# A fifth Strassen block pair in ten of the eleven gate and up tiles of a decoder layer's second FFN, with its weight sums made during keys and queries

## The chip, the core and the metric

The kernel runs on one core of one Trainium2 chip, with float32 inputs and outputs. The metric is the device time of one execution in microseconds; the time before is the median of three runs. Five engines matter in the text: PE (TensorE, matmuls), DVE (VectorE), ACT (ScalarE), POOL (GpSimd, which here issues transfers and does a few small operations) and SP (SyncE, which issues most transfers). Each runs its own instructions in order; semaphores tie them together.

## The reference

One layer of a decoder with 256 tokens and 16 meta tokens ahead of them, width 2048. What the change touches is the last line; keys and queries are part of `mixer`.

```python
h = h + 0.5 * swiglu(rms_norm(h, g1), w_gate1, w_up1, w_down1)   # D_FF = 5632
u = rms_norm(h, g_mix)                                           # mixer: attention + short conv
h = h + merged(u) @ w_out
h = h + 0.5 * swiglu(rms_norm(h, g2), w_gate2, w_up2, w_down2)
# swiglu(x, g, u, d) = (silu(x @ g) * (x @ u)) @ d
```

## The kernel before

**Products.** Each weight block comes from memory in float32. ACT copies it to a rounded high half `whi` (line 175), DVE subtracts this from the block and so makes the low half `wlo` (line 176). A product is then three matmuls: high by high, high by low, low by high (lines 374 to 376, 402 to 404 and 408 to 410). `Stream` (class at line 105) keeps all weights in one list: loads of up to 1 MB into `raw` buffers (issued by SP at line 152), and splits of up to 1024 columns. One split is one **step**: `next` runs what is due at the step, makes the split three steps ahead, runs what is due behind it (`waiting`), and hands out the blocks. Functions are put in with a step number by `later`, `early` and `put`, so that number sets the order on DVE, ACT and POOL. There are four buffers for split halves, so the split of step n+4 waits until PE has used that of step n. In the second FFN there are four raw buffers (`raw` three times, `raws` once); a load goes out when the load four places ahead has been split.

**Stages.** First FFN; keys and values (steps 0 to 9 of the second stage), index queries (10 to 25), queries (26 to 41); convolution, eight columns of six steps each (from 42); gates and branches; output product; second FFN. While the convolution runs, the steps' list also holds the top-k selection (`top`), the queries' scaling and rotation (`scaled`, `rotation`), the turn of the queries into the tile `qT` (line 1135) and the scores (line 1208).

**Second FFN.** The tokens are two halves of 128; gate and up weights come in tiles of 512 + 512 columns, 6 in the first group and 5 in the second (`GROUPS`), each followed by its down product in two halves. A tile runs over 2048 inputs as eight **pairs** of 128-row blocks, counted from 0. A plain pair is 2 steps of four products (24 matmuls). A Strassen pair (`MIXED`, in tiles other than the first: 1, 3, 5 and 6) is 4 steps, A, B, C, D, with 2, 1, 2 and 2 products (21 matmuls): seven products of sums of token halves with sums of weight blocks. A and B use three of the four weight blocks as they are (a load of 768 KB), C and D use four sums of weight blocks (a load of 1 MB). The sums of activations lie in tiles such as `comb`; `act_combos` makes them.

**Weight sums.** The sums are made ahead of time by **jobs** (`job`, lines 554 to 573): POOL loads 1 MB, DVE makes four sums of 128x512 in place, one at a step, POOL stores the result to a scratch tensor (`made`, or `sums` for down weights). 46 jobs run during the first FFN, the other 11 during gates and branches, every 5 or 6 steps.

**Between tiles.** The gated result of a tile is turned block by block (`turn_gated`), stored to `hold`, read back as `mt` in four pieces of 128 KB by POOL's queue (`move_blocks`, lines 645 and 648) while the next tile runs, and split into `mid`.

`FIVE` lists the tiles in which pair 4 (`FIFTH`) is a Strassen pair, too; before, it is empty.

Of the kernel before, what the change touches and what calls it, by code (L numbers as in the profile page):

```python
# [9 lines left out]
F32 = mybir.dt.float32  # L10
# [59 lines left out]
FIFTH = 4  # L70
FIVE = ()
LAST_MORE = 3, 4
JOBS_FROM = 24
JOBS_EVERY = 5
JOBS = 46
LATE_FROM = 4
LATE_EVERY = 6
# [5 lines left out]
    act_combos=(4, 12, 19, 32), factors=(7, 10, 12), out=(1, 1, 5, 17), act_split=(9, 14, 25, 33),  # L83
    below=(12, 17, 22, 30, 34), below_split=(15, 20, 30, 34, 35), fifth=(22, 25), late_below=(0, 5),
    late_split=(0, 6),
# [150 lines left out]
def tile_decoder_layer(  # L236
# [316 lines left out]

    def job(pool, bufs, src, to, at, every, touch):
        box = {}

        def load():
            box["x"] = pool[0].tile([P, RAW], F32, name="made", bufs=bufs)
            if touch:
                nc.vector.tensor_copy(box["x"][:, :1], ones[:, :1])  # L560
            nc.gpsimd.dma_start(box["x"], src)

        def sums(n):
            b12, b11, b22, b21 = (box["x"][:, i * HALF : (i + 1) * HALF] for i in range(4))
            to, a, b, op = (
                (b22, b22, b12, "sub"), (b12, b12, b11, "sub"), (b11, b22, b11, "add"), (b21, b21, b11, "sub")
            )[n]
            getattr(nc.vector, f"tensor_{op}")(to, a, b)  # L568

        st.later(load, 1, at)  # L570
        for n in range(4):
            st.later(lambda n=n: sums(n), 1, at + every + n)
        st.later(lambda: nc.gpsimd.dma_start(to, box["x"]), 1, at + every + 4)

    def ffn_features():
# [3 lines left out]
        with tc.tile_pool(name="ffn1", bufs=2, reuse_waits="tile") as fp:  # L579
# [15 lines left out]

            for i, (src, to) in enumerate(made[:JOBS]):
                job([fp], 3, src, to, st.at + JOBS_FROM + i * JOBS_EVERY - 1, JOBS_EVERY, i < 3)

# [55 lines left out]
    def ffn_tokens():  # L654

        with ExitStack() as pools:
# [209 lines left out]
            for g, n in enumerate(GROUPS):  # L866
                for f in range(n):
# [11 lines left out]
                    if (g, f) == (g, 1 - g) and any(at[0] == g for at in FIVE):  # L879
                        written.discard("fifth")  # L880
                        fns = combos(halves, FIFTH, [below[:, 1, :1], below[:, 0]], "fifth")
                        put(fns, 5 * (LAG["fifth"][0],) + 4 * (LAG["fifth"][1],))
                    quads(c, m, lambda k, j, part: known(("act", k // 4), act_tokens(k, j, part)), now, 8, lambda m=m: put(spread(m), LAG["spread"]))
# [67 lines left out]
    with ExitStack() as mix:  # L951
# [6 lines left out]
        qiT = mp.tile([P, 8, SEQ], F32, name="qiT", tag="tA")  # L958
        qT = mp.tile([P, H, SEQ], F32, name="qT", tag="tB")
        ys = mp.tile([P, H, 2, SEQ], F32R, name="ys")  # L960
        cs = [mp.tile([P, KC // 2, 2, SEQ], F32R, name=f"cs{i}", tag=f"c{i}") for i in range(2)]
        vts = mp.tile([P, 4, G * HD], F32, name="vts", tag="vts")
# [239 lines left out]
        def scores(p, lag):  # L1202
            px = aux_tile("psc")
            for a in range(2):
                hh = 2 * p + a
                for j in (1, 2):
                    at = META * (2 - j)
                    nc.tensor.matmul(
                        px[:, a, SIDE[j]],
                        qT[:, hh, (j - 1) * P : j * P],  # L1210
                        kall[:, hh // (H // G), at : at + SEEN[j]],
# [69 lines left out]


        def q_steps():
            left = len(steps)
# [11 lines left out]
            new += [prep[3], tops[3], prep[4], tops[4], visit(prep[5], tops[5]), tops[6]]  # L1296
            new += [visit(*[lambda j=j: turn(qT, j) for j in (1, 2)]), tops[7], mask]
            for i in range(left):
# [46 lines left out]
        def conv_b(c, pb, y):  # L1345
            t = mw.tile([P, SEQ], F32, name="t", tag="cy")
            joined(t, pb)
            nc.vector.tensor_mul(y, t, y)
            to = cs[c // 4][:, c % 4]
            split_into(to[:, 0, :], to[:, 1, :], y)  # L1350

        for c in range(KC):
            box = {}
# [21 lines left out]
        st.later(jobs_pool, 3)  # L1375
        for i, (src, to) in enumerate(made[JOBS:]):
            job(jobs, 2, src, to, st.at + LATE_FROM + i * LATE_EVERY, LATE_EVERY, i < 2)

# [236 lines left out]
```

## Time and profile before

| what | us |
|---|---|
| median of three runs | 2108.76 (2107.89 to 2109.12) |
| span of the profiled execution | 2106.9 |
| PE busy in it | 2098.8 |
| DVE busy | 1582.4 |
| ACT busy | 1058.9 |
| keys to the last convolution column | 788 to 1070 |
| gate and up tiles and down products of the second FFN | 1419 to 2101 |

The profile records one execution; the span goes from its first to its last instruction. A row of a timeline gives the start, the duration, the engine, the line and the operation, with what ended the idle time ahead of it in brackets. A row of a windows' view gives PE, weight loads, DVE, ACT and POOL in this order, busy us with the number of instructions, then PE's clock (1.00 throughout), the mean share of the DMA engines and GB/s. A row of issues gives the size and the median time from issue to landing. Matmuls overlap, so the distance of two starts is less than a matmul's duration.

### The profile page before, as it was taken

Reading aid. Unit: us, or ns where it says so; the run is one execution under the profiler, and the core shown is the slowest. Engines: PE = TensorE matmul, PEld = TensorE weight load, DVE = VectorE, ACT = ScalarE, POOL = GpSimd, SP = SyncE. Lnnn points to the kernel's source line nnn. Section 1 sums busy time; section 2 is a strip of 40 time slices with the busy share of each in tenths; the row PEclk is TensorE's granted clock in tenths of the full one; section 3 lists DMA queues with packets and bytes.
Section 4 is the critical chain, followed back from the end, with each engine's and each line's share of the span. In section 5 each row is a group of like instructions: output and inputs, shape, how many; then the busy total and the mean of one; then the engine's idle time right before and its main releaser. Section 6 shows DMA issues by size and latency. Waiting matters only on the chain.

```text
span 2106.9 us, 31863 instructions
## 1 busy us (share of the span) xinstructions
PE 2098.8 (100%) x12731; PEld 1889.9 (90%) x12731; DVE 1582.4 (75%) x2144; ACT 1058.9 (50%) x1342; POOL 106.0 (5%) x207
## 2 busy tenths in 40 slices
PE   9999999999999999999999999999999999999998
PEld 9999999999999999889988888888888888888887
DVE  7676766676776766578679678769788896878897
ACT  6444433344444445565444444456575565566654
POOL 0000000000000000000000000011000000000000
PEclk9999999999999999999999999999999999999999
DMA  7788888888888865445468886667988777799865
GB/s 265 260 320 327 324 315 322 311 337 310 322 313 325 328 224 177 164 159 181 152 216 329 323 301 223 219 233 255 314 314 300 281 268 247 282 306 319 306 250 207
DMA packets 85908, 575.64 MB, mean 273 GB/s; under 512 B 10112, under 2 KB 10880, under 8 KB 23808
## 3 DMA queue, kind: packets, MB, share of 16 engines
q1 hardware_dynamic: 64080, 438.34, 58.4%
q0 software_dynamic: 21104, 134.23, 17.1%
q8 instruction: 99, 1.62, 0.3%
q10 hardware_dynamic: 576, 1.05, 0.1%
q14 instruction: 49, 0.40, 0.1%
HBM read 504.90 MB, written 68.68 MB: 272 GB/s over the span
## 4 chain that ended last, share of the span: by engine, by line
PE 98%; DVE 1%; DMA 1%; issue 0%; ACT 0%; DVEq 0%; ACTq 0%
PE three L409 5%; PE three L408 5%; PE three L410 5%; PE pd L375 4%; PE pd L376 4%; PE pd L374 4%; PE pu L374 4%; PE pg L375 4%; PE pg L374 4%; PE pu L375 4%; PE pg L376 4%; PE pu L376 4%; PE pgt L402 3%; PE pgt L404 3%; PE pgt L403 3%; PE one L408 3%
## 5 line engine op out<-in xcount | busy, mean ns | idle before, releaser
L176 DVE TENSOR_TENSOR wlo<-raw,whi 128x1024 fp32r<-128x1024 f32 (+1 forms) x771 | 906.2, 1188 | 464.5 <-ACT whi L175 457.7
L175 ACT ACTIVATE whi<-raw 128x1024 fp32r<-128x1024 f32 (+1 forms) x771 | 786.4, 1030 | 883.4 <-PE pd L375 146.2
L375 PE MATMUL pd<-mid,whi 128*128 128x272 f32 x704 | 201.9, 287 | 0.0
L376 PE MATMUL pd<-mid,wlo 128*128 128x272 f32 x704 | 201.9, 287 | 0.0
L374 PE MATMUL pd<-mid,whi 128*128 128x272 f32 x704 | 201.9, 287 | 0.0
L374 PE MATMUL pu<-act,whi 128*128 128x272 f32 x672 | 192.8, 287 | 0.0
L376 PE MATMUL pu<-act,wlo 128*128 128x272 f32 x672 | 192.7, 287 | 0.0
L376 PE MATMUL pg<-act,wlo 128*128 128x272 f32 x672 | 192.7, 287 | 0.0
L375 PE MATMUL pg<-act,whi 128*128 128x272 f32 x672 | 192.7, 287 | 0.0
L375 PE MATMUL pu<-act,whi 128*128 128x272 f32 x672 | 192.7, 287 | 0.0
L374 PE MATMUL pg<-act,whi 128*128 128x272 f32 x672 | 192.7, 287 | 0.0
L568 DVE TENSOR_TENSOR made<-made 128x512 f32<-128x512 f32 x228 | 156.3, 685 | 0.0
L408 PE MATMUL three<-whi,act 128*128 128x512 f32 x352 | 137.2, 390 | 0.1
L409 PE MATMUL three<-wlo,act 128*128 128x512 f32 x352 | 137.0, 389 | 0.0
L410 PE MATMUL three<-whi,act 128*128 128x512 f32 x352 | 137.0, 389 | 0.0
L376 PEld LDWEIGHTS pd<-mid,wlo 128*128 128x128 f32 x704 | 132.7, 188 | 0.0
L374 PEld LDWEIGHTS pd<-mid,whi 128*128 128x128 f32 x704 | 132.7, 188 | 0.0
L375 PEld LDWEIGHTS pd<-mid,whi 128*128 128x128 f32 x704 | 132.7, 188 | 0.0
L176 DVE TENSOR_TENSOR wlo<-raws,whi 128x1024 fp32r<-128x1024 f32 x92 | 103.5, 1140 | 31.7 <-ACT whi L175 31.0
L374 PEld LDWEIGHTS pu<-act,whi 128*128 128x128 f32 x672 | 126.7, 188 | 0.0
L374 PEld LDWEIGHTS pg<-act,whi 128*128 128x128 f32 x672 | 126.7, 188 | 0.0
L376 PEld LDWEIGHTS pg<-act,wlo 128*128 128x128 f32 x672 | 126.6, 188 | 0.0
(381 smaller groups left out, 4482.7 us busy)
## 6 DMA issues: line engine op xcount, KB each, us to landing
raw<-in_wgu_dram SPq DMA_DIRECT2D x123, 1024.0 KB, 6.4
raw<-in_wd_dram SPq DMA_DIRECT2D x63, 1024.0 KB, 6.7
made<-in_wgu_dram POOLq DMA_DIRECT2D x41, 1024.0 KB, 10.6
made<-made POOLq DMA_DIRECT2D x41, 1024.0 KB, 6.5
raw<-made SPq DMA_DIRECT2D x31, 1024.0 KB, 6.1
raw<-in_wcv_dram SPq DMA_DIRECT2D x24, 1024.0 KB, 4.9
raw<-in_wgc_dram SPq DMA_DIRECT2D x24, 1024.0 KB, 5.1
raw<-in_wga_dram SPq DMA_DIRECT2D x24, 1024.0 KB, 5.4
```

The costliest lines, as they stand in the source:

```text
L175: nc.scalar.activation(hi[:, :n], raw, AF.Copy)
L176: nc.vector.tensor_sub(lo[:, :n], raw, hi[:, :n].bitcast(F32))
L374: nc.tensor.matmul(ps, whi, xhi, start=first, stop=False)
L375: nc.tensor.matmul(ps, whi, xlo, start=False, stop=False)
L376: nc.tensor.matmul(ps, wlo, xhi, start=False, stop=last)
L402: nc.tensor.matmul(ps, xhi, whi, start=k + i == 0, stop=False)
L403: nc.tensor.matmul(ps, xhi, wlo, start=False, stop=False)
L404: nc.tensor.matmul(ps, xlo, whi, start=False, stop=k + i == n - 1)
L408: nc.tensor.matmul(ps, x(0), w[0], start=first, stop=False)
L409: nc.tensor.matmul(ps, x(0), w[1], start=False, stop=False)
L410: nc.tensor.matmul(ps, x(1), w[0], start=False, stop=last)
L568: getattr(nc.vector, f"tensor_{op}")(to, a, b)
```

## The change

`FIVE` now lists the tiles 1 to 5 of the first group and all five of the second, so pair 4 of these tiles is a Strassen pair, and the Strassen pairs of a tile are 1, 3, 4, 5, 6. That makes ten more jobs. The list of jobs stays in the order of use: the first 46 still run in the first FFN, the last 11 during gates and branches, and ten in between now run from step 3 of the second stage, one every five steps. Job i (from 0) loads at step 3 + 5i, makes its sums at steps 8 + 5i to 11 + 5i, and stores at step 12 + 5i. Its buffer is the place of the tile `cs1` (even i, tag c1) or of `qT` (odd i, tag tB); these tiles are now created when they are first written, `qT` at step 58 and `cs1` in the convolution's fifth column. The activations' sums for pair 4 go into `below`; their nine operations (five adds, two ACT copies, two subtractions) are put at other steps of the first tile that needs them.

```diff
-FIVE = ()
+FIVE = (*((0, f) for f in range(1, GROUPS[0])), *((1, f) for f in range(GROUPS[1])))
...
+MID_JOBS = 10
+MID_FROM = 3
+MID_EVERY = 5
...
-    below=(12, 17, 22, 30, 34), below_split=(15, 20, 30, 34, 35), fifth=(22, 25), late_below=(0, 5),
+    below=(12, 17, 22, 30, 34), below_split=(15, 20, 30, 34, 35), fifth=(5, 5, 7, 7, 9, 11, 11, 13, 13), late_below=(0, 5),
...
-    def job(pool, bufs, src, to, at, every, touch):
+    def job(place, src, to, at, every, touch):
...
-            box["x"] = pool[0].tile([P, RAW], F32, name="made", bufs=bufs)
+            box["x"] = place()
...
-                        put(fns, 5 * (LAG["fifth"][0],) + 4 * (LAG["fifth"][1],))
+                        put(fns, LAG["fifth"])
...
-        qT = mp.tile([P, H, SEQ], F32, name="qT", tag="tB")
+        late_tiles = {}
...
-        cs = [mp.tile([P, KC // 2, 2, SEQ], F32R, name=f"cs{i}", tag=f"c{i}") for i in range(2)]
+        for i, (src, to) in enumerate(made[JOBS : JOBS + MID_JOBS]):
+            job(
+                lambda i=i: mp.tile([P, RAW], F32, name="made", tag=("c1", "tB")[i % 2]), src, to,
+                st.at + MID_FROM + i * MID_EVERY, MID_EVERY, i < 2,
+            )
...
+        def place_q():
+            late_tiles["qT"] = mp.tile([P, H, SEQ], F32, name="qT", tag="tB")
...
-        for i, (src, to) in enumerate(made[JOBS:]):
-            job(jobs, 2, src, to, st.at + LATE_FROM + i * LATE_EVERY, LATE_EVERY, i < 2)
+        for i, (src, to) in enumerate(made[JOBS + MID_JOBS :]):
```

SP's queue in tile 1 of the first group, before: the loads of pair 3 (weights, then sums, `made11`), the whole load of pair 4, weights and sums of pairs 5 (`made13`) and 6 (`made14`), and the load of pair 7.

```order
L152 DMA raws_14326<-in_wgu2_dram 128x1536
L152 DMA raw_14724<-made11_76 128x2048
L152 DMA raw_14770<-in_wgu2_dram 128x2048
L152 DMA raw_14789<-in_wgu2_dram 128x1536
L152 DMA raws_14326<-made13_77 128x2048
L152 DMA raw_14844<-in_wgu2_dram 128x1536
L152 DMA raw_14863<-made14_78 128x2048
L152 DMA raw_14885<-in_wgu2_dram 128x2048
```

The same place in the changed program (columns are 128 partitions by elements; 2048 are 1 MB, 1536 are 768 KB):

```order
L155 DMA raws_14408<-in_wgu2_dram 128x1536
L155 DMA raw_14806<-made11_76 128x2048
L155 DMA raw_14852<-in_wgu2_dram 128x1536
L155 DMA raw_14875<-made12_77 128x2048
L155 DMA raws_14408<-in_wgu2_dram 128x1536
L155 DMA raw_14935<-made13_78 128x2048
L155 DMA raw_14954<-in_wgu2_dram 128x1536
L155 DMA raw_14976<-made14_79 128x2048
L155 DMA raws_14408<-in_wgu2_dram 128x2048
```

Pair 4's whole load has become a load of 768 KB and one of 1 MB, and four pairs in a row now bring 1.75 MB each.

DVE in the first columns of the convolution, before: three splits, with a round of top-k, the convolution's first product (`cx`) and the end of a rotation between them.

```order
L176 TENSOR_TENSOR wlo<-raw,whi 128x1024
L1186 MAX m_10359<-keys 128x8
L1187 MATCH_REPLACE keys<-m_10359,keys 128x272
L176 TENSOR_TENSOR wlo<-raw,whi 128x1024
L1325 TENSOR_TENSOR cx<-pxc,few 128x258
L999 TENSOR_TENSOR zz_8894<-rot 128x8x16
L1000 TENSOR_TENSOR zz_8894<-rot 128x8x16
L1186 MAX m_10396<-keys 128x8
L1187 MATCH_REPLACE keys<-m_10396,keys 128x272
L176 TENSOR_TENSOR wlo<-raw,whi 128x1024
```

The same place in the changed program:

```order
L179 TENSOR_TENSOR wlo<-raw,whi 128x1024
L571 TENSOR_TENSOR made<-made 128x512
L1196 MAX m_10431<-keys 128x8
L1197 MATCH_REPLACE keys<-m_10431,keys 128x272
L179 TENSOR_TENSOR wlo<-raw,whi 128x1024
L571 TENSOR_TENSOR made<-made 128x512
L1340 TENSOR_TENSOR cx<-pxc,few 128x258
L1009 TENSOR_TENSOR zz_8904<-rot 128x8x16
L1010 TENSOR_TENSOR zz_8904<-rot 128x8x16
L1196 MAX m_10469<-keys 128x8
L1197 MATCH_REPLACE keys<-m_10469,keys 128x272
L179 TENSOR_TENSOR wlo<-raw,whi 128x1024
```

A sum of the ninth job stands behind each of these splits; the tenth job's four sums stand in the same way behind four splits a little later.

ACT at the copy of the turned queries into `qT`, before, with what each row waits for:

```order
L175 ACTIVATE whi<-raw 128x1024 [waits PE_49,Activation_49]
L1135 ACTIVATE qT<-pqt 128x8x128 [waits PE_49] x2
L175 ACTIVATE whi<-raw 128x1024 [waits DMAHW2_49,DVE_49,PE_49]
L1333 ACTIVATE cy<-cx,small 128x256 [waits DVE_49]
L175 ACTIVATE whi<-raw 128x1024 [waits PE_49,Activation_49]
```

The same place in the changed program (DMASW are transfers that POOL issued):

```order
L178 ACTIVATE whi<-raw 128x1024 [waits PE_49,Activation_49]
L1145 ACTIVATE qT<-pqt 128x8x128 [waits DMASW4_49,DMASW1_49,DMASW5_49,DMASW0_49,DMASW7_49,DVE_49,PE_49]
L1145 ACTIVATE qT<-pqt 128x8x128 [waits PE_49]
L178 ACTIVATE whi<-raw 128x1024 [waits DMAHW2_49,PE_49,Activation_49]
L1348 ACTIVATE cy<-cx,small 128x256 [waits DVE_49]
```

The first copy now also waits for transfers of the jobs that used its place.

More of the change, by code (lines that the diff above doesn't have):

```diff
@@ L596, in ffn_features @@
             for i, (src, to) in enumerate(made[:JOBS]):
-                job([fp], 3, src, to, st.at + JOBS_FROM + i * JOBS_EVERY - 1, JOBS_EVERY, i < 3)
+                job(
+                    lambda: fp.tile([P, RAW], F32, name="made", bufs=3), src, to,
+                    st.at + JOBS_FROM + i * JOBS_EVERY - 1, JOBS_EVERY, i < 3,
+                )
             two = [aux_tile(f"start{i}") for i in range(2)]
@@ L958, in tile_decoder_layer @@
         qiT = mp.tile([P, 8, SEQ], F32, name="qiT", tag="tA")
-        qT = mp.tile([P, H, SEQ], F32, name="qT", tag="tB")
+        late_tiles = {}
         ys = mp.tile([P, H, 2, SEQ], F32R, name="ys")
-        cs = [mp.tile([P, KC // 2, 2, SEQ], F32R, name=f"cs{i}", tag=f"c{i}") for i in range(2)]
+        for i, (src, to) in enumerate(made[JOBS : JOBS + MID_JOBS]):
+            job(
+                lambda i=i: mp.tile([P, RAW], F32, name="made", tag=("c1", "tB")[i % 2]), src, to,
+                st.at + MID_FROM + i * MID_EVERY, MID_EVERY, i < 2,
+            )
         vts = mp.tile([P, 4, G * HD], F32, name="vts", tag="vts")
@@ L1209, in scores @@
                         px[:, a, SIDE[j]],
-                        qT[:, hh, (j - 1) * P : j * P],
+                        late_tiles["qT"][:, hh, (j - 1) * P : j * P],
                         kall[:, hh // (H // G), at : at + SEEN[j]],
@@ L1296, in q_steps @@
             new += [prep[3], tops[3], prep[4], tops[4], visit(prep[5], tops[5]), tops[6]]
-            new += [visit(*[lambda j=j: turn(qT, j) for j in (1, 2)]), tops[7], mask]
+            new += [visit(
+                place_q, *[lambda j=j: turn(late_tiles["qT"], j) for j in (1, 2)]
+            ), tops[7], mask]
             for i in range(left):
@@ L1348, in conv_b @@
             nc.vector.tensor_mul(y, t, y)
+            if c % 4 == 0:
+                cs.append(mp.tile([P, KC // 2, 2, SEQ], F32R, name=f"cs{c // 4}", tag=f"c{c // 4}"))
             to = cs[c // 4][:, c % 4]
             split_into(to[:, 0, :], to[:, 1, :], y)
+        cs = []
         for c in range(KC):
@@ L1375, in tile_decoder_layer @@
         st.later(jobs_pool, 3)
-        for i, (src, to) in enumerate(made[JOBS:]):
-            job(jobs, 2, src, to, st.at + LATE_FROM + i * LATE_EVERY, LATE_EVERY, i < 2)
+        for i, (src, to) in enumerate(made[JOBS + MID_JOBS :]):
+            job(
+                lambda: jobs[0].tile([P, RAW], F32, name="made", bufs=2), src, to,
+                st.at + LATE_FROM + i * LATE_EVERY, LATE_EVERY, i < 2,
+            )
         m = [mp.tile([P, 2, 2, 512], F32, name=f"m{i}", tag=t) for i, t in enumerate(("tA", "tB"))]
```

## The prediction

> **What bounds the kernel now.** I read the page's busy table first, then the chain that ended last, then the windows of the two stages that the change touches.
>
> ```profile
> span 2106.9 us, 31863 instructions
> PE 2098.8 (100%) x12731; PEld 1889.9 (90%) x12731; DVE 1582.4 (75%) x2144; ACT 1058.9 (50%) x1342; POOL 106.0 (5%) x207
> PE 98%; DVE 1%; DMA 1%; issue 0%; ACT 0%; DVEq 0%; ACTq 0%
> ```
>
> PE works without a gap and is 98% of the chain, so a matmul less is time less, and every wait that the change puts in front of PE is time more. What can put one there is DVE (it makes `wlo`, the low half of each weight block) and the DMA (it brings the blocks). So I ask in each touched stage how far ahead of PE they are. The profiled execution's span is 2106.9 us; the median of the runs is 2108.76 us, and the 1.9 us between them lies outside the first and the last instruction. The sum is made on the span and carried over to the median. What a measurement of this kernel can tell from no change is 0.2%, 4.2 us.
>
> **The gain.** The next row is the window of five gate and up tiles of the second FFN, from the start of tile 1 to the start of the down product: 902 matmul starts in 204.20 us.
>
> ```profile
> 1461.78:1665.98 204.20, 204.20 (x902) 169.00 (x900) 170.46 (x176) 130.06 (x146) 13.69 (x25) 1.00 0.88 310
> ```
>
> One matmul is 204.20 / 902 = 0.2264 us; the 390 ns that the page gives each overlap. A pair of blocks takes 24 matmuls, by Strassen's products 21. Ten tiles get one more such pair: 30 matmuls less, 30 x 0.2264 = **6.8 us less**. That is certain as long as PE stays fed.
>
> DVE is busy 170.46 us of the 204.20, 34.1 of 40.8 in a tile. A Strassen pair brings 3.5 weight splits of 1024 columns in place of 2, about 1.7 us of DVE more at the 1.13 us from one to the next (second fence below, 1799.06: three in 3.49). That gives 35.8 us in a tile of 40.2: DVE stays under PE, and this part I cost at nothing by itself.
>
> **Ten more jobs during keys and queries.** Each job loads 1 MB, makes four sums on DVE and stores 1 MB. Up to some 935 us I see no cost: as in the first of the next rows, DVE is idle for half of the time and the transfers have the room, which hides the sums and the jobs' loads. Behind it, in the convolution's first columns, DVE is the late one:
>
> ```profile
> 920.00:930.00 10.00, 10.00 (x81) 9.77 (x81) 3.93 (x10) 7.43 (x30) 0.00 (x0) 1.00 0.30 107
> 940.00:950.00 10.00, 10.00 (x74) 9.40 (x73) 9.34 (x22) 7.51 (x14) 0.20 (x1) 1.00 0.48 152
> 950.00:960.00 10.00, 10.00 (x83) 9.86 (x83) 9.34 (x18) 2.95 (x5) 0.74 (x1) 1.00 0.55 186
> 960.00:970.00 10.00, 10.00 (x72) 9.25 (x71) 9.86 (x22) 6.62 (x9) 0.00 (x0) 1.00 0.64 217
> ```
>
> The third number with an (x) in a row is DVE's: 3.9 of 10 us first, then 9.3 to 9.9. The last two jobs, and the end of the one before, put ten sums into this stretch, two ahead of 937 us and eight behind it, one behind each of several splits (the order in the section on the change). What one adds is read from two equal adds in a row, and what DVE has in hand from the splits and the matmuls that need them (DVE first, then PE, then the ACT copy and the scores):
>
> ```profile
> 1504.31 0.68 DVE L781 TENSOR_TENSOR u<-one,u 128x512 f32<-128x512 f32 x1
> 1504.91 0.68 DVE L782 TENSOR_TENSOR u<-two,u 128x512 f32<-128x512 f32 x1
> ...
> 936.10 1.23 DVE L982 TENSOR_TENSOR zz<-zz,small 128x1024 f32<-128x1024 f32 x1 [0.42 <-ACT zz L981]
> 943.91 1.22 DVE L176 TENSOR_TENSOR wlo<-raw,whi 128x1024 fp32r<-128x1024 f32 x1
> 956.75 1.21 DVE L176 TENSOR_TENSOR wlo<-raw,whi 128x1024 fp32r<-128x1024 f32 x1
> 962.98 1.22 DVE L176 TENSOR_TENSOR wlo<-raw,whi 128x1024 fp32r<-128x1024 f32 x1
> 965.34 2.35 DVE L176 TENSOR_TENSOR wlo<-raw,whi 128x1024 fp32r<-128x1024 f32 x2
> ...
> 945.58 0.28 PE L386 MATMUL pb<-act,wlo 128*128 128x256 f32 x1
> 959.80 0.28 PE L376 MATMUL pcg<-act,wlo 128*128 128x258 f32 x1
> 970.08 0.28 PE L376 MATMUL pxc<-act,wlo 128*128 128x258 f32 x1
> 972.72 2.98 PE L1208 MATMUL psc<-keys,qT 128*128 128x144 f32 x16
> ...
> 963.53 1.92 ACT L1135 ACTIVATE qT<-pqt 128x1024 f32<-128x1024 f32 x2
> ```
>
> An add of 512 columns costs its successor 0.60 us. The split that ends at 943.91 + 1.22 = 945.13 is used at 945.58: 0.45 in hand. The next ones: 957.96 against 959.80, 1.84 in hand; 966.56 (the first of the two at 965.34) against 970.08, 3.52 in hand. Ahead of these three stand 3, 7 and 10 sums: 1.8, 4.2 and 6.0 us, less the 0.42 that DVE waits at 936.10 today. So the splits come 0.9, 1.9 and 2.1 us late, and as waits of one queue don't add up, PE loses the largest: **2.1 us**.
>
> Then the tile `qT`. It takes the place of the odd jobs' buffer, so ACT's copy into it waits until the last job's store has landed. The last sum stands behind the split at 962.98: 962.98 + 1.13, with nine sums ahead of it (5.0) makes 969.1, its end 969.8. For the store, the nearest rows are a late job's store and the load behind it, on POOL:
>
> ```profile
> 1158.60 0.54 POOL L573 DMA_DIRECT2D sums<-made  x1 [10.22 <-DVE made L568]
> 1163.23 0.53 POOL L561 DMA_DIRECT2D made<-in_wd_dram  x1 [4.10 <-DMA sums<-made]
> ```
>
> From a store to what waits for its landing: 4.6 us. So the copies start at 974.5 and the second ends 1.9 us later, 976.4 to 976.6, against scores due at 972.72 + 2.1 = 974.8: **1.7 us** more. Queued behind the waiting copy on ACT are the next `whi` split and the convolution's first tap, and behind them DVE; the following split is due on PE only when the scores' 2.6 us are over, which covers them. In all 3.8 us; from below 1 (the sums find gaps that I don't see, and the store lands first), from above 6 (the store takes the 6.5 us of the page's `made<-made` row instead of 4.4).
>
> ```profile
> made<-made POOLq DMA_DIRECT2D x41, 1024.0 KB, 6.5
> ```
>
> **The sums of act blocks for the fifth pair** are made twice, in the first tile of each group that uses them: five adds and four split halves. Two of the adds now stand behind the split at 1799.06 in the second group:
>
> ```profile
> 1799.06 3.49 DVE L176 TENSOR_TENSOR wlo<-raw,whi 128x1024 fp32r<-128x1024 f32 x3
> 1801.93 0.39 PE L409 MATMUL one<-wlo,act 128*128 128x512 f32 x1
> L703 DVE TENSOR_TENSOR few<-few x13: 291/292/294, 1428.5 to 2059.2; 128x128 f32<-128x128 f32 x13
> ```
>
> The second of the three splits ends at 1801.4 and is used at 1801.93, 0.5 in hand; an add of 512 columns and one of 128 take 0.6 + 0.3: **0.4 us** late, from 0 to 0.8 for both groups.
>
> **The weights of four Strassen pairs in a row.** Pairs 3, 5, 6 become 3, 4, 5, 6. Such a pair needs 0.75 MB of weights and 1 MB of sums (1.835 million bytes) in 21 x 0.2264 = 4.75 us: 386 GB/s, while the whole tile asks for 310 today and about 335 then. The run begins where the transfers are worst: the 128 KB pieces that turn the tile before (`mt<-hold`) stand between the loads. In the tile that starts at 1873.18 and in the one that starts at 1584.30, the weights and the sums of pair 5 took (issue rows of the first tile, then the landings of both tiles):
>
> ```profile
> 1873.18 0.39 PE L408 MATMUL one<-whi,act 128*128 128x512 f32 x1
> 1883.77 0.33 SPq L152 DMA_DIRECT2D raw<-in_wgu_dram  x1
> 1885.51 0.33 SPq L152 DMA_DIRECT2D raws<-made  x1
> ...
> raw<-in_wgu_dram SPq DMA_DIRECT2D x1, 768.0 KB, 10.1
> raws<-made SPq DMA_DIRECT2D x1, 1024.0 KB, 11.2
> ...
> raw<-in_wgu_dram SPq DMA_DIRECT2D x1, 768.0 KB, 8.6
> raws<-made SPq DMA_DIRECT2D x1, 1024.0 KB, 10.0
> ```
>
> They were issued 10.6 and 12.3 us behind the tile's start and landed at 20.7 and 23.5 there, at 19.2 and 22.3 in the other tile. How late a load may land is shown by one that came too late, in the last down product (the chain, in order of time):
>
> ```profile
> 2072.36 8.25 DMA raw<-sums
> 2080.72 1.07 ACT whi L175
> 2081.81 1.24 DVE wlo L176
> 2083.09 0.50 PE three L409
> ...
> L409 PE MATMUL three<-wlo,mid 128*128 128x512 f32 x176 | 68.7, 391 | 1.1 <-DVE wlo L176 1.1
> L408 PE MATMUL three<-whi,mid 128*128 128x512 f32 x176 | 68.6, 390 | 0.3 <-ACT whi L175 0.3
> ```
>
> From the landing (2080.61) to the matmul 2.48 us; and such a miss costs up to 1.4 us (the idle times of the two groups, which hold all down products). It happened in a run of five Strassen pairs. Now the new order: pair 4's weights and sums go at the places of the old whole load and of pair 5's weights, the same 1.75 MB, so its sums land when pair 5's weights land now, 19.2 to 20.7, or up to 0.8 later if the slowest of the 16 engines is charged with the longer piece (a quarter of the 2.8 to 3.1 us between the two landings). Their first matmul is the 99th of the tile, their `wlo` is due at 22.4 + 0.2, so they must land by 20.2: the one tile has 0.2 to 1.0 in hand, the other is 0.5 to 1.3 late. Pair 5's weights land 0.25 MB sooner than the old second piece, at 21.7 to 22.9, and must by 22.9; its sums, 2.5 us behind (1 MB at some 420 GB/s, the fullest slices below), at 24.2 to 25.4, and must by 24.9. Behind pair 6 come two unmixed pairs, in which the queue recovers. So a tile like the one at 1584.30 loses nothing and keeps 0.7 us, one like that at 1873.18 about 1 us. I take five tiles of the slow kind at 0.8 and 1.5 us for a load or two that is slow by chance, **5.5 us**; bounds 0 (all tiles as the good one) and 14 (1.4 in each of ten).
>
> The slices of a window over two tiles (2.1 us each) show the ceiling:
>
> ```profile
> GB/s 57 315 17 278 357 226 362 306 225 249 312 416 428 420 166 386 348 319 224 389 368 145 193 414 237 381 246 292 259 333 419 408 411 104 239 391 353 332 355 341
> ```
>
> Runs of slices at 408 to 428 lie above the 386 that the run asks for. [...]
>
> **Sum:** -6.8 + 3.8 + 0.4 + 5.5 = +2.9 us: span 2109.8, time 2108.76 + 2.9 = **2111.7 us**.
>
> **Rivals.** *The covers hold* (faster): no wait in the convolution or at `qT`, and the loads come in time; then -6.8 + 0.4 = -6.4, 2102.4 us. For it speaks that the down products, which have three Strassen pairs in a row in each half, show no more idle time on PE than those 1.4 us; against it DVE at 9.3 to 9.9 of 10 in the convolution, which leaves the ten sums no room. It needs less than 2.6 us of waits in all; chance 0.12. *The run of four is starved in every tile* (slower): the loads' rate in the run, not the single slow tile, decides; each of ten tiles pays what the miss in the run of five paid, 1.4: -6.8 + 4.2 + 14 = +11.4, 2120.2 us. It decides from about 0.7 us a tile on (waits over 11 us in all). For it speaks that today's tiles land pair 5's loads with less than 1 us to spare and the kernel has four raw buffers, two pairs' worth; against it the fullest slices. Chance 0.38. *Nothing changes in the program* is excluded: the order has 30 matmul rows less. The forecast, waits that eat the gain within 4.2 us either way, has 0.50.
>
> **Numbers.** The range reaches from 2104.5 (waits of 2.5 us) to 2119 (17 us, near the starved case), which leaves about one in ten out at each end. Faster by over 0.2%: 0.12, within: 0.50, slower: 0.38.
>
> **What would show it.** Right: 30 fewer matmuls at the same 0.2264 us; PE idle or long matmuls at the scores, released by ACT's `qT`, which waits for `made`'s store; `wlo` as releaser of PE in the convolution at 945 to 972; in the tiles, `whi` waiting for `raw<-made` and PE for `wlo` in pairs 4 and 5, in half of the tiles. Wrong: PE without idle time in these places (then it is faster), or idle time in all ten tiles, or a DVE that is late in the run while its data is there.

## The result and the profile after

The changed kernel takes 2133.46 us (median of four runs, 2130.45 to 2135.48) against 2108.94 us before (2107.89 to 2109.24): ratio 1.0116, 95% interval 1.0102 to 1.0131. It is 1.2% slower, and the forecast of 2111.7 us and its range up to 2119 are both left behind. The top of its profile page and the shares of the chain that ended last:

```profile
span 2131.4 us, 31993 instructions
PE 2107.8 (99%) x12701; PEld 1881.6 (88%) x12701; DVE 1627.6 (76%) x2220; ACT 1073.0 (50%) x1366; POOL 117.5 (6%) x227
...
PE 75%; DVE 12%; DMA 9%; issue 3%; ACT 2%; DVEq 0%; ACTq 0%; SPq 0%
```

PE was 98% of the chain and is now 75% of it. It has 30 matmuls fewer and is yet busy 9.0 us longer: part of the lost time stands in matmul records that last longer (397 ns in the mean for `three` at L412, 389 for the same products before), the rest is idle time. The 24.5 us of span split as follows: the second FFN begins at 1430.10 and not at 1418.94 (11.2 later), its ten tiles with a fifth pair take 13.7 us longer, the rest is -0.3. The windows of the two groups of five tiles, first of the kernel before (its first group stands in the prediction), then of the changed one:

```profile
1791.11:1995.70 204.59, 204.46 (x901) 168.96 (x900) 170.68 (x176) 126.91 (x141) 10.98 (x20) 1.00 0.87 306
```

```profile
1472.94:1685.46 212.52, 207.18 (x887) 164.12 (x885) 180.50 (x192) 137.21 (x158) 13.70 (x25) 1.00 0.89 315
1810.86:2020.81 209.95, 205.54 (x886) 164.65 (x885) 180.57 (x192) 134.21 (x153) 10.96 (x20) 1.00 0.88 315
```

Ten tiles: 408.79 us before, 422.47 now, with 30 matmuls fewer. At 0.2264 us a matmul they would be 407.5 and 400.7 without a stall; so stalls, the time by which matmul starts fall behind that pace, went from 1.3 to **21.7 us**. Rows of the changed kernel's list of waits (us in total, times, the longest) tell who is late:

```profile
ACT whi L178 <- DMA raw<-made: 21.3, 18, 2.5
ACT qT L1145 <- DMA made<-made: 11.1, 1, 11.1
PE three L412 <- DVE wlo L179: 7.3, 19, 0.8
PE psc L1218 <- ACT qT L1145: 3.0, 2, 2.8
PE three L411 <- DVE u L776: 2.8, 4, 1.2
PE pqt L1141 <- DVE zz L1010: 1.6, 1, 1.6
PE pb L389 <- DVE wlo L179: 1.0, 1, 1.0
```

**Ahead of the second FFN.** Read in order of time, PE falls behind the kernel before by 0.6 us up to 830 us (0.2 of it stands there before the first of the ten jobs), by 1.9 at the late splits in the convolution up to 954 (the row of `pb` is one), by 0.6 at another late split at 962.87, by 1.9 where the transposes of the queries (`pqt`) wait for DVE's rotation of `zz`, and by 5.0 at the scores. Here the chain of the changed kernel around the scores:

```profile
967.22 0.60 DVE made L571
...
970.25 0.61 DVE made L571
970.86 0.29 issue
971.15 8.34 DMA made<-made
979.80 0.71 issue
980.52 1.03 ACT qT L1145
981.59 4.14 PE psc L1218 x14
```

The last sum ends at 970.86, its store takes 8.34 us, and only then may ACT write `qT`. The scores, 16 matmuls in 2.98 us before, take 0.71 for the first two and 4.14 for the other 14; the window of this stretch has the reason in the column ahead of the DMA share:

```profile
980.00:985.00 5.00, 4.12 (x14) 3.23 (x15) 2.42 (x5) 4.18 (x6) 0.19 (x1) 0.66 0.04 13
```

The granted clock was 0.66 in the mean: PE had stood for 2.79 us, and then a record of 0.5 begins, which lasts 3.41 us.

**In a tile.** The chain of the changed kernel in the tile that starts at 1894.52:

```profile
1906.20 10.21 DMA raw<-made
...
1916.51 1.07 ACT whi L178
...
1921.71 2.88 DVE wlo L179 x3
1924.59 0.02 issue
1924.61 7.58 DMA raws<-in_wgu_dram
...
1932.29 1.07 ACT whi L178
...
1934.53 0.68 DVE u L774
```

Pair 4's sums go out 11.7 us behind the tile's start and land at 21.9, where the prediction wanted them by 20.2. That makes their split late. But a split also frees a buffer: the load at 1924.61, the next tile's first, goes out 0.02 us behind the split that frees its place. So lateness goes round: late landing, late split, late issue of the load four places on, late landing. And at the tile's turn DVE has little room to make it good: in the kernel before it works without a gap from 1908.72, 5.3 us ahead of the tile's start at 1914.02, and has pair 1's C ready 0.56 us before PE needs it (the first of the four splits in the second row, used at 1921.7):

```profile
1908.72 1.22 DVE L176 TENSOR_TENSOR wlo<-raws,whi 128x1024 fp32r<-128x1024 f32 x1
...
1919.99 4.59 DVE L176 TENSOR_TENSOR wlo<-raw,whi 128x1024 fp32r<-128x1024 f32 x4
```

This was read from the trace. Whether DVE or the transfers are the root, and what about the transfers, is what the experiments are for.

### The profile page after: what moved, and what is told of

It reads as the page before. It is cut to its first block, busy times and chain, and to the rows that moved or that the text cites. A ratio compares the mean times of both kernels' runs of the same rounds, so it can differ in the third digit from the quotient of the medians.

```text
span 2131.4 us, 31993 instructions
## 1 busy us (share of the span) xinstructions
PE 2107.8 (99%) x12701; PEld 1881.6 (88%) x12701; DVE 1627.6 (76%) x2220; ACT 1073.0 (50%) x1366; POOL 117.5 (6%) x227
## 4 chain that ended last, share of the span: by engine, by line
PE 75%; DVE 12%; DMA 9%; issue 3%; ACT 2%; DVEq 0%; ACTq 0%; SPq 0%
DVE wlo L179 7%; PE pd L379 4%; PE pd L377 4%; PE pd L378 4%; PE pu L378 4%; PE pg L378 4%; PE pu L379 4%; PE pg L379 4%; PE pg L377 4%; PE pu L377 4%; DMA raw<-in_wgu_dram 3%; PE pgt L407 3%; PE pgt L406 3%; PE pgt L405 3%; DMA raw<-made 2%
## 5 line engine op out<-in xcount | busy, mean ns | idle before, releaser
L179 DVE TENSOR_TENSOR wlo<-raw,whi 128x1024 fp32r<-128x1024 f32 (+1 forms) x785 | 919.4, 1184 | 451.6 <-ACT whi L178 446.1
L178 ACT ACTIVATE whi<-raw 128x1024 fp32r<-128x1024 f32 (+1 forms) x785 | 796.6, 1026 | 844.6 <-PE pd L378 144.4
L571 DVE TENSOR_TENSOR made<-made 128x512 f32<-128x512 f32 x268 | 183.5, 685 | 0.1
L412 PE MATMUL three<-wlo,act 128*128 128x512 f32 x342 | 135.6, 397 | 2.5 <-DVE wlo L179 2.3
L411 PE MATMUL three<-whi,act 128*128 128x512 f32 x342 | 133.8, 391 | 2.9 <-DVE u L776 2.8
L413 PE MATMUL three<-whi,act 128*128 128x512 f32 x342 | 133.4, 390 | 0.0
L179 DVE TENSOR_TENSOR wlo<-raws,whi 128x1024 fp32r<-128x1024 f32 x98 | 108.1, 1127 | 24.3 <-ACT whi L178 22.9
L379 PEld LDWEIGHTS pu<-act,wlo 128*128 128x128 f32 x672 | 126.6, 188 | 0.0
```

Of the source, the lines that this page charges most:

```text
L178: nc.scalar.activation(hi[:, :n], raw, AF.Copy)
L179: nc.vector.tensor_sub(lo[:, :n], raw, hi[:, :n].bitcast(F32))
L379: nc.tensor.matmul(ps, wlo, xhi, start=False, stop=last)
L411: nc.tensor.matmul(ps, x(0), w[0], start=first, stop=False)
L412: nc.tensor.matmul(ps, x(0), w[1], start=False, stop=False)
L413: nc.tensor.matmul(ps, x(1), w[0], start=False, stop=last)
```

## The experiments

Two theories. **Transfers**: the loads of the run of four Strassen pairs are late, DVE passes it on. **DVE**: its 1.7 us of added splits per tile are what doesn't fit. In the table, "begin" is the start of the second FFN against 1418.94 (what the jobs cost), "ten tiles" their time by the windows (408.79 before). Kernels without the ten jobs begin 0.0 to 0.9 us later, so less than 1 us in that column tells nothing.

| run | median us | ratio, 95% interval | begin | ten tiles |
|---|---|---|---|---|
| changed kernel | 2133.46 | 1.0116 (1.0102 to 1.0131) | +11.2 | 422.5 |
| e1 jobs only | 2119.91 | 1.0053 (1.0037 to 1.0070) | +11.6 | 409.4 |
| e2 fifth pair only | 2123.68 | 1.0074 (1.0059 to 1.0089) | +0.2 | 421.9 |
| e3 its loads small | 2115.67 | 1.0035 (1.0022 to 1.0048) | +0.5 | 414.0 |
| e4 low halves on POOL | 2126.26 | 1.0081 (1.0066 to 1.0097) | +0.4 | 428.1 |
| e5 all loads small | 2103.45 | 0.9972 (0.9962 to 0.9983) | +0.1 | 402.5 |
| e6 low halves on ACT | 2122.62 | 1.0062 (1.0047 to 1.0077) | +0.9 | 423.8 |
| e7 late turn | 2128.20 | 1.0092 (1.0074 to 1.0109) | +0.2 | 428.4 |
| e8 jobs swapped | 2114.28 | 1.0023 (1.0014 to 1.0033) | +6.2 | 409.7 |
| e9 late halves | 2149.22 | 1.0195 (1.0178 to 1.0212) | +19.6 | 427.9 |
| e10 pair 2 | 2144.74 | 1.0172 (1.0156 to 1.0187) | +2.5 | 441.1 |
| e11 pieces at the turn | 2138.02 | 1.0140 (1.0125 to 1.0155) | +18.8 | 419.3 |
| e12 no pieces | 2111.09 | 1.0011 (1.0002 to 1.0020) | +0.1 | 411.8 |
| e13 half buffers | 2104.07 | 0.9981 (0.9971 to 0.9990) | +2.8 | 403.4 |
| e14 all pieces at the turn | 2114.20 | 1.0029 (1.0017 to 1.0042) | +3.0 | 409.1 |
| e15 pieces and halves | 2104.32 | 0.9982 (0.9973 to 0.9992) | +2.2 | 402.0 |
| e16 before, half buffers | 2107.36 | 0.9996 (0.9986 to 1.0006) | 0.0 | 408.9 |

Where the ten tiles stall, us by pair (matmul starts, less 0.2264 per matmul):

| kernel | 0 | 1 | 2 | 3, 4 | 5 | 6 | 7 | sum |
|---|---|---|---|---|---|---|---|---|
| changed | 4.7 | 4.5 | 0.9 | 6.5 | 1.7 | 2.5 | 1.0 | 21.7 |
| e2 | 2.6 | 4.2 | 0.9 | 6.2 | 4.3 | 2.3 | 0.7 | 21.2 |
| e3 | 0.7 | 4.2 | 0.8 | 0.1 | 0.7 | 5.2 | 1.5 | 13.2 |
| e5 | 0.1 | 0.1 | 0.9 | 0.1 | 0.1 | 0.4 | 0.1 | 1.7 |
| e7 | 1.3 | 0.1 | 0.1 | 0.1 | 23.3 | 2.4 | 0.4 | 27.7 |
| e11 | 2.2 | 0.1 | 0.1 | 0.1 | 0.8 | 15.0 | 0.3 | 18.5 |
| e12 | 3.4 | 4.2 | 0.9 | 0.1 | 0.1 | 2.4 | 0.1 | 11.1 |
| e13 | 0.1 | 0.7 | 1.1 | 0.1 | 0.1 | 0.5 | 0.1 | 2.7 |

**e1 and e2: one part alone.** In e1 the tiles keep their four Strassen pairs; in e2 pair 4's sums are not made and the blocks themselves are loaded.

```diff
 e1
-            for i, name in order(8, now):
+            for i, name in order(8, MIXED if gu else FIRST_MIXED):
...
 e2
-            sums = {i: scratch.tile([P, RAW], F32, name=f"made{gu + i}") for i in now}
+            sums = {i: scratch.tile([P, RAW], F32, name=f"made{gu + i}") for i in now if i != FIFTH}
-                st.add_part(name, wgu2[gu + i], sums.get(i))
+                st.add_part(name, wgu2[gu + i], sums.get(i, wgu2[gu + i]))
...
-MID_JOBS = 10
+MID_JOBS = 0
```

> The ten jobs run during keys, queries and convolution as in the changed kernel, but no tile uses their sums: the gate and up tiles have the four Strassen pairs of before. If the losses of the two stages add up, as the two traces say (second FFN begins 11.2 us later than before, its tiles lose 14 on balance), this kernel takes 2108.9 + 11 = about 2120 us, with waits at the transposes and the copies of the queries. If the jobs' delay is absorbed later or the tiles' stalls need both parts, it lies nearer to the 3.8 us of the prediction: 2113.

> The ten tiles take pair 4 by Strassen's products, but its four sums are not made: the blocks themselves are loaded in their place (same size, same queue), so the ten jobs fall away and the result is not the layer's. If the tiles lose by themselves, 2108.9 - 6.8 + 21 = 2123 us, with the stalls at pair 4's C and at the next tile's pairs 0 and 1. If the tiles stall only because the jobs came first, about 2103 to 2108.

2119.91 and 2123.68: 11.7 and 15.5 us over the 2108.18 of before on that chip, 27.2 together against the change's 24.5. Each part loses by itself and where the traces said. In e2, 5 us slices of a tile (start 1884.01; the last columns are clock, DMA share, GB/s) show how uneven the transfers are: they are busy for less than half of the time when a tile begins, since no load goes out from 1882.9 until a split frees a buffer at 1888.8, and have no room 15 us later:

```profile
1885.00:1890.00 5.00, 5.00 (x23) 4.09 (x24) 4.96 (x7) 2.29 (x3) 0.00 (x0) 1.00 0.43 166
...
1900.00:1905.00 5.00, 5.00 (x23) 4.14 (x23) 3.36 (x4) 2.64 (x3) 0.00 (x0) 1.00 1.02 277
```

**e3 and e5: smaller loads, the same splits.** In e3 pair 4's two loads have 512 KB each; in e5 all loads of the tiles have (`small` for every pair). The blocks that are not loaded are left out of the products, and others are used twice.

```diff
+        if small and name in "BD":            # e5: "1BD"
+            a, b = 0, b - a
...
-            self.own = load(src if name == "0" else src[:, HALF:]), name == "A" and load(made)
+            x = src[:, 2 * HALF :] if small else src if name == "0" else src[:, HALF:]
+            self.own = load(x), name == "A" and load(made[:, : 2 * HALF] if small else made)
```

> As the run with the fifth pair alone, but pair 4's two loads bring 512 KB each in place of 768 KB and 1 MB: C and D use the same two blocks, B one of A's. The tile then moves as many bytes as before, while DVE makes all its splits. The result is not the layer's. Theory of the transfers (late loads of the run of four pairs delay DVE, which then is late in the next tile, too): nearly all of the 21 us of stalls go, 2103 to 2107 us. Theory of DVE (1.7 us of splits more in a tile is what it cannot do in time): the stalls at pair 4 and at the next tile's start stay, 2117 to 2123 us.

> As the run with the fifth pair alone, but every load of a gate and up tile brings 512 KB, so the transfers can never be late; DVE, ACT and PE do the same instructions. The result is not the layer's. If the transfers are the root of all stalls and DVE only passes them on, nearly nothing of the 21 us stays: 2102 to 2104 us. If DVE's work at a tile's turn (the sums of products, the gate, the turned blocks, ahead of pair 1's C) is a bound of its own that the fifth pair pushes over, the 4 us at pair 1's C and the 0.8 behind it stay: 2106 to 2109 us.

e3 fits neither number: the stalls of pairs 4 and 5 go, those of pair 1 stay and pair 6's grow. e5 settles it: 2103.45 us, with stalls of 1.7 us. DVE does in it what it does in e2 (180.5 us in each group there) and has the room:

```profile
1461.84:1662.84 201.00, 201.00 (x887) 166.03 (x886) 180.37 (x192) 138.72 (x158) 13.69 (x25) 1.00 0.66 205
1788.31:1989.76 201.45, 201.15 (x886) 165.96 (x885) 180.42 (x192) 135.43 (x153) 10.96 (x20) 1.00 0.65 198
```

180.4 us of DVE in 201.0 and no stall at pair 1's C: the theory of DVE as the root falls, its lateness there is the transfers' passed on.

**e4 and e6: less work for DVE** (both on e2): the two low halves of the gated result, 128x512 each, are made by POOL in e4, and replaced by plain copies on ACT in e6.

```diff
-                        lambda x=x, hi=hi, lo=lo: nc.vector.tensor_sub(lo, x(), hi.bitcast(F32)),
+                        lambda x=x, hi=hi, lo=lo: nc.gpsimd.tensor_sub(lo, x(), hi.bitcast(F32)),   # e4
+                        lambda x=x, lo=lo: nc.scalar.activation(lo, x(), AF.Copy),                  # e6
```

> As the run with the fifth pair alone, but the two subtractions per tile that make the low half of the gated result run on POOL: DVE loses some 1.3 of the 1.7 us that the fifth pair adds, just behind pair 4's C, and the loads stay. Theory of DVE: most of the stalls behind pair 4 go, 2108 to 2114 us. Theory of the transfers: pair 4's C is as late as before and so is the next tile's start, 2120 to 2124 us.

> As the run with the fifth pair alone, but the two low halves of the gated result per tile are written by ACT (a plain copy, so the result is not the layer's) and no longer by DVE: 1.2 us of DVE less per tile behind pair 4's C, without POOL beside it. The loads stay. If DVE's lack of room behind a late load is what carries the lateness into the next tile, the stalls at pairs 5 and 6 and at the next tile's pairs 0 and 1 (about 12 of 21 us) fall by half or more: 2112 to 2118 us. If it is the transfers alone, about 2122 us as with the fifth pair alone.

e6 gains nothing (its interval overlaps that of e2), as the theory of the transfers says. e4, at 2126.26, lies above both of its numbers and tells nothing on the question, since DVE's splits last longer beside POOL's work. POOL's group in e4 (mean ns behind the comma):

```profile
L819 POOL TENSOR_TENSOR mid<-mt,mid 128x512 fp32r<-128x512 f32 x18 | 32.3, 1792 | 119.6 <-ACT mid L818 107.4 <-PE one L413 12.2
```

DVE's row in e4 beside one of these subtractions, which ran from 1956.14 to 1957.96:

```profile
1955.58 2.94 DVE L179 TENSOR_TENSOR wlo<-raws,whi 128x1024 fp32r<-128x1024 f32 x2 [0.63 <-ACT whi L178]
```

Both splits are one of 1024 and one of 512 columns. The same pair in the kernel before:

```profile
1924.50 1.82 DVE L176 TENSOR_TENSOR wlo<-raws,whi 128x1024 fp32r<-128x1024 f32 x2
```

**e7: the last tile's turn four steps later**, with its move and halves (on e2). Here, and in e9, e11, e14 and e15, the sums of activations for the fifth pair come a few steps later, too.

```diff
-turn=(1, 1), move=4, hi=(28, 33), lo=(28, 33)
+turn=(9, 9), move=10, hi=(32, 37), lo=(32, 37)
```

> As the run with the fifth pair alone, but the turning of the last tile's gated result (1.3 us of DVE) stands behind pair 1's and pair 2's splits, four steps later, with its move and its halves moved by as much. Theory of DVE at the tile's turn: the 4 us at pair 1's C go, 2117 to 2120 us. Theory of the transfers alone: the turned blocks' pieces now meet the loads of the run of four pairs later in the tile, so the stalls stay about as large or change place, 2121 to 2128 us.

The stalls change place: pairs 1 and 4 lose theirs, pair 5 gets 23.3 us. The pieces now land late, and ACT waits for them with the weights' splits queued behind:

```profile
ACT mid L818 <- DMA mt<-hold: 13.0, 6, 6.0
```

**e8: odd and even jobs change places** (on e1), `tag=("tB", "c1")[i % 2]`.

> As the run with the jobs alone, but odd and even jobs change places: the last job now lies in the place of cs1, and the tile of the turned queries waits only for the last job but one, whose store goes out five steps (some 10 us) earlier. If the scores' delay (5 us in the trace of the changed kernel, with the lower clock behind it) comes from that store, this kernel is 4 to 5 us faster than the jobs alone: 2115 us. If DVE's late splits and rotation are what the scores wait for anyway, it gains under 1.5 us: 2119 us.

5.6 us less than e1. In e1 and e8 the list of waits has:

```profile
ACT qT L1139 <- DMA made<-made: 10.7, 1, 10.7
PE psc L1212 <- ACT qT L1139: 2.8, 2, 2.4
PE pqt L1135 <- DVE zz L1004: 1.6, 1, 1.6
PE pb L389 <- DVE wlo L179: 1.0, 1, 1.0
```

```profile
PE pqt L1135 <- DVE zz L1004: 1.6, 1, 1.6
PE pb L389 <- DVE wlo L179: 1.0, 1, 1.0
```

In e8 PE loses nothing at the scores: the store in front of `qT` is worth 5 us, with what the clock of 0.5 costs in it (3.41 us stand at that clock in the changed kernel). What the sums on DVE make late stays, 4.5 us at the splits and the rotation.

**e9, e10, e11: other schedules, with all the work.** The jobs get a third place, `tag=("c1", "tB", "c0")[i % 3]`, and come every 3 steps (e9, e11) or 4 (e10, and e13 to e15 below). e9 is the late turn with `hi=(44, 47), lo=(44, 47)`; e10 has `FIFTH = 2`, so Strassen pairs 1, 2, 3, 5, 6; e11 stores the turned blocks at step 7 and reads them back by SP at the tile's last step:

```diff
-turn=(1, 1), move=4, hi=(28, 33), lo=(28, 33)
+turn=(13, 13), move=14, back=50, hi=(60, 61), lo=(60, 61)
...
+    def back_blocks(x, hold, queue):          # queue: nc.sync
+        of_quarter = hold.rearrange("(r f) q j c -> q f r (j c)", r=4)
+        for q in range(4):
+            queue.dma_start(x[q * 32 : q * 32 + 32], of_quarter[q])
```

> The changed kernel with all its work, and two edits in two stages. Jobs: one every three steps over three places (c1, tB and, new, the place of cs0), so the last store goes out 18 steps earlier, ahead of the convolution; if DVE's late splits, rotation and the last store make up the 11.2 us ahead of the second FFN, 0 to 3 us stay there; if the jobs cost by their transfers or their DVE time as such, 8 or more. Tiles: the late turn again, with the two halves of the gated result 14 steps behind the place they had with the late turn, so nothing waits for the turned pieces: of the 28 us of stalls with the late turn those at pair 5's B, C and D (23 us) fall to about 8 if ACT's wait for the pieces made them, and stay over 15 if the loads of pair 5, slowed by the pieces, made them. In all about 2108.9 + 2 - 6.8 + 12 = 2116 us.

> The changed kernel with pair 2 by Strassen's products in place of pair 4: runs of three and of two Strassen pairs, with a plain pair between, and the same bytes and splits in a tile. Jobs over three places, every four steps. If a run of four is what starves the tile, its 21 us of stalls fall to 6 or less; if the tile's total of transfers against its time does it, they stay about 20, and move to pairs 2 and 3 and to pair 1's C, since no plain pair stands behind the tile's turn. Jobs: 1 to 4 us ahead of the second FFN. In all 2108.9 + 3 - 6.8 + 6 to 20 = 2111 to 2125 us.

> The changed kernel with all its work. Jobs as in the run with late halves: 0 to 3 us. Tiles: the turned blocks are stored six steps into the next tile and their four pieces read back, on SP's queue, only at that tile's last step, where the transfers idle (the first 5 us of a tile have a DMA share of 0.43 in the run with the fifth pair alone, the next 35 us 0.91 to 1.02); their halves are made in the tile behind it. No byte is saved. If the pieces' place among the loads of the run of four is the root of the stalls, these fall from 21 to 5 us or less: about 2108.9 + 2 - 6.8 + 4 = 2108 us, with both parts of the change kept. If the loads are too much for the run even without the pieces, 12 us or more stay: 2116 us and over.

Every 4 steps the jobs cost 2.2 to 3.0 us (0.9 of it at a late split, nothing at the rotation and the scores); every 3 steps they cost 19, more than the change's own, where 0 to 3 were expected. There a job's load waits for the store of the job three ahead, and DVE, in order, for the load. So e9 takes 2149 us where 2116 were expected, e11 2138 where 2108 were. The waits of e9:

```profile
POOL made L564 <- DMA made<-made: 78.8, 10, 12.5
DVE made L571 <- DMA made<-in_wgu_dram: 20.3, 4, 6.2
```

In e9, 27 us of stalls stay (pair 5's fall to 6, pairs 0 and 6 get 6 and 14). e10 is worse: 40 us of stalls, at pairs 2 and 3 and at the plain pair 4, whose load comes behind a run of three (by estimate, up to 10 of the 40 us are the clock's, which stood at 0.5 for 20.5 us in these tiles):

```profile
ACT whi L178 <- DMA raw<-in_wgu_dram: 28.5, 14, 4.9
```

So it doesn't take a run of four. In e11 pairs 1 to 5 are nearly clear, and pair 6 stalls for 15 us; half of all stalls (9.2 us) stand in the two tiles whose pieces still went out in mid-tile.

**e12 to e15: pieces, or the time of issue?** e12 leaves the pieces' round trip out (on e2; the `move_blocks` line removed). e13 keeps all the work and the places of the pieces and makes eight buffers of 512 KB of the four of 1 MB, with one load for each split; e14 is e11 with all pieces at the turn, the turn of a group's last tile up to a step later, and jobs every 4 steps; e15 is both.

```diff
 e13
-        if name in "0A":
-            self.own = load(src if name == "0" else src[:, HALF:]), name == "A" and load(made)
-        g = self.own[name in "CD"]
-        a, b = {"0": (0, 2), "1": (2, 4), "A": (0, 2), "B": (2, 3), "C": (0, 2), "D": (2, 4)}[name]
+        a, b = {"0": (0, 2), "1": (2, 4), "A": (1, 3), "B": (3, 4), "C": (0, 2), "D": (2, 4)}[name]
+        g = load((made if name in "CD" else src)[:, a * HALF : b * HALF])
...
+            while self.freed < self.kept:
+                h = self.halves.pop(self.freed, None)
+                if h is None:
+                    x = self.raw_pool.tile([P, RAW], F32, name="raw")
+                    self.free += [x[:, :SUB], x[:, SUB:]]
+                else:
+                    self.free.append(h)
+                self.freed += 1
+            while self.n_loaded < len(self.loads) and self.free:
+                self.load_one()
 e14
-at = (15, 44, 47) if f == n - 2 else (LAG["back"], *LAG["hi"])
+at = (46, 56, 58) if f == n - 2 else (LAG["back"], *LAG["hi"])
```

> As the run with the fifth pair alone, but the round trip of the turned blocks in gate and up tiles is left out (no store to hold, no four pieces back; the halves are made of the blocks as they lie, so the result is not the layer's). All weights and sums of weights are loaded as before. If it is the round trip among the loads that starves the run of four, the 21 us of stalls fall to 4 or less: 2106 us or under. If the weights' own bytes with four buffers are too much for the run, 12 us or more stay: 2114 us or more.

> The changed kernel with all its work, jobs over three places every four steps (2.5 us ahead of the second FFN, as in the run with pair 2). In the second FFN each 1 MB buffer serves as two of 512 KB, one load per split: the same bytes and the same SBUF, but a load goes out when half a buffer is free, about 1.1 to 1.4 us sooner for every second half. If the loads are late because they are issued late, the 21 us of stalls fall to 10 or less: 2108.9 + 2.5 - 6.8 + 10 = 2115 us or under. If the engines that move them are full, they stay near 20: 2124 to 2128 us.

> The changed kernel with all its work; jobs every four steps (2.5 us), pieces read back at each tile's last step as in the run with the pieces at the turn, now also for the last tile but one of each group, whose pieces there went out in the middle of the run (3.2 and 6.0 us of stalls in those two tiles). 18.5 us of stalls fall by these 9 to about 10: 2108.9 + 2.5 - 6.8 + 10 = 2115 us. If stalls only move to the next place, it stays at 18: 2123 us.

> The last two edits together: pieces at the turn in all tiles, and half buffers. If late issue and the pieces' place make up the stalls, 5 us or less stay and the kernel is level with before: 2108.9 + 2.5 - 6.8 + 4 = about 2109 us. If the transfers' total is the bound, 12 us or more stay: 2117 us.

Without the pieces 11.1 us of stalls stay, between the two numbers: the pieces make pairs 4 and 5 late, not the tile's end. Pair 1's C still stalls for about 0.5 us in eight of the ten tiles, so the lateness that goes round doesn't need a late pair 4. In e13, with the same bytes and the pieces in their old place, 2.7 us of stalls are left; its ten tiles:

```profile
1465.55:1667.50 201.95, 201.78 (x886) 165.84 (x885) 182.52 (x194) 139.00 (x158) 13.71 (x25) 1.00 0.93 332
1792.63:1994.08 201.45, 201.13 (x886) 165.96 (x885) 181.44 (x193) 135.49 (x153) 10.95 (x20) 1.00 0.92 328
```

At 0.93 of the engines' time and 332 GB/s the transfers keep up, where they failed at 0.89 and 315. Two things changed: a load goes out when half a buffer is free, and a split needs its own half only. SP's issues of the sums of pairs 4, 5 and 6, in the changed kernel (tile start 1894.52) and in e13 (1873.60):

```profile
1906.20 0.33 SPq L155 DMA_DIRECT2D raw<-made  x1
...
1913.44 0.33 SPq L155 DMA_DIRECT2D raws<-made  x1
...
1920.00 0.33 SPq L155 DMA_DIRECT2D raw<-made  x1
```

```profile
1883.05 1.46 SPq L154 DMA_DIRECT2D raws<-made  x2
...
1889.07 3.05 SPq L154 DMA_DIRECT2D raw<-made  x2
...
1895.19 1.68 SPq L154 DMA_DIRECT2D raws<-made  x2
```

11.7, 18.9 and 25.5 us behind the tile's start there; here the first halves at 9.5, 15.5 and 21.6. In these two tiles the whole loads landed at 21.9, 26.4 and 31.4; here the first halves, which are all that C's split needs, land at 14.9, 23.2 and 27.5, the second at 18.9, 24.5 and 28.8. So the first halves go out 2.2, 3.4 and 3.9 us sooner and land 7.0, 3.2 and 3.9 us sooner: at pairs 5 and 6 the earlier issue is all of it, at pair 4 less than a third. No run takes the two apart.

In the changed kernel the engines that move the loads were 0.88 to 0.89 busy, and the tiles became shorter all the same in e13: with its loads of 256 and 512 KB the ten tiles take 19 us less than with those of 768 KB and 1 MB. e14 (8.4 us of stalls) shows that the pieces' place is worth something, too; e15 adds nothing to e13 that the time shows.

**e16: the half buffers without the change.**

> The kernel before with the half buffers alone: four Strassen pairs per tile, no jobs added. Its tiles have 1.3 us of stalls, so if the half buffers only keep the loads of the run of four in time, there is nothing for them to gain here: 2107 to 2110 us, no change. If they make the kernel faster by themselves (the same 4 us as with the fifth pair), the fifth pair would not be what the gain comes from: 2104 us.

No change: the ten tiles have nothing to win,

```profile
1464.16:1668.64 204.48, 204.48 (x901) 168.85 (x900) 171.19 (x177) 130.77 (x146) 13.74 (x25) 1.00 0.92 307
1793.78:1998.20 204.42, 204.42 (x902) 168.85 (x901) 170.24 (x176) 127.39 (x141) 11.00 (x20) 1.00 0.90 304
```

and what the last down product wins by them (56.2 us from its start to the end, 58.2 before) the first tile loses (45.25 against 42.84). So e13's gain needs both: ten tiles 5.4 us shorter, the last down product 2.0, against 2.8 for the jobs and 0.95 in the first tile, 3.7 us in all. e13, at 0.9981 (0.9971 to 0.9990), is faster than the kernel before by 0.2% and than the changed one by 1.3%, by the two ratios; its interval and that of e16 just touch.

## Why the prediction was wrong, step by step

**The gain, -6.8 us: right.** With the loads out of the way (e5) the ten tiles take 402.45, 6.3 less than before, and the sums for the fifth pair's activations cost the 0.4 us foreseen: the first tiles of the two groups stall 0.3 and 0.8 us there, 0.1 and 0.5 before.

**The jobs, 3.8 us with bounds 1 to 6: wrong, 11.2.** The late splits, "PE loses the largest: 2.1 us", were right in size with 1.9 and 0.6, but a second one did add to the first. "From a store to what waits for its landing: 4.6 us" was one row taken for the price: the store took 8.34 us, the scores lost 5.0 us where 1.7 were foreseen. Of the 5.0, up to 1.7 are the lower clock's, by an estimate from half of the 3.41 us at 0.5 (from the first score to the next product 4.69 us against 2.61, with a wait of 0.20 in it). The stretch of that row was not much quieter, 0.89 of the engines' time and 334 GB/s from 1158.0 to 1163.3 against 0.98 and 348 in the 8.35 us here; but there the load ahead of the store landed 1.4 us after the store went out, and here it had gone out only 0.9 us before the store. How much of the difference this makes no run shows. And the rotation of `zz`, which stands behind the same sums on DVE, wasn't in the sum at all: 1.9 us. The rest of the 11.2 is 0.6 us up to 830 us and 1.1 us in steps of some 0.16 at the gates, branches and the output product; the steps are there in all runs with the ten jobs and in none without them, and no run tells why.

**The run of four, 5.5 us with bounds 0 to 14: wrong, 20.0 us** (stalls 21.7 against 1.3, less the 0.4 above). Three steps failed. The landing of pair 4's sums was foreseen for 19.2 to 21.5 us; it came at 21.0 to 23.4 in seven tiles, and at 17.6 to 19.9 only in the first of each group and the last of the second. "Behind pair 6 come two unmixed pairs, in which the queue recovers": it doesn't, because a load goes out only when a split frees its buffer, so late splits issue late loads, into the next tile. "DVE stays under PE, and this part I cost at nothing by itself" is true by itself (e5), but at the tile's turn DVE has 0.56 us to spare, and so hands on all lateness above that; 9.2 of the 21.7 us stand in pairs 0 and 1, behind the turn, which the prediction didn't look at.

**The rival that came nearest** is "the run of four is starved in every tile" with its 2120.2 us, given 0.38. Its side was right, all ten tiles stall, but not its mechanism: it is not the loads' mean rate, since the changed kernel stalled at 315 GB/s and e13 goes at 332 with 2.7 us of stalls, and it takes no run of four (e10). It is the size of the buffers, which sets when a load goes out and how much must land before a split. A prediction that multiplied one miss by ten tiles could not find this; following one late load to the next load's issue would have shown where to look.

## What to carry to other kernels

Where a buffer is freed by the work that waits for it, a late load makes the next loads late (21.7 us of stalls in the changed kernel); ask of a load not only when it lands but what lets it go out and how much of it the first split needs, and try smaller buffers of the same total (2.7 us of stalls in e13) before moving work about. One row is not a price: a store of 1 MB took 4.3 us in one place and 8.34 in another, with the engines 0.89 and 0.98 busy, so let the bounds reach over what else may be in flight. After the engine that waits, read what else stands behind the added work on the same in-order queue: here the rotation behind the sums cost 1.9 us, the splits 2.5.

## What the runs showed of the hardware

**PE's clock fell behind some stands of 2 to 5 us.** In the changed kernel a record of 0.5 lasts 3.41 us from 980.85, behind a stand of 2.79 us that ends at 980.67; in e7 a stand of 4.88 us is followed by 6.83 us at 0.5. Stands of 1.65 us (from 966.63) and 1.21 us (from 1514.81) in the changed kernel left the clock at 1.00; in e10 one of 1.97 us had a fall behind it and one of 2.36 had none. A record of 0.5 costs PE up to half its length, by an estimate from e10, where matmuls start 0.43 us apart in it in place of 0.2264: 1.7 us for the 3.41, and 3.4 us for the 6.83 that follow the stand of 1.97 us in e10.

**POOL beside DVE.** In e4 a 128x512 subtraction on POOL took 1.79 us in the mean, and a pair of DVE's splits beside one took 2.94 us, against 1.82 in the kernel before.
